# A dot-product modulation spread over three stages and block sums moved to VectorE, in a two-layer hybrid encoder

## The chip, the cores and the metric

The kernel runs on one core of one Trainium2 chip. The metric is the device time of one execution in microseconds; the reported time is the median of several runs. Below, PE is TensorE, DVE is VectorE, ACT is ScalarE, POOL is GpSimd, and SP issues most DMAs.

## The reference, cut to what matters

A two-layer encoder over 1024 positions and 1024 channels, all in float32. Each layer has a mixer (attention in the first, a long convolution called hyena in the second) and a feed-forward part. Six vectors per layer (shift, scale and gate of both parts) come from the conditioning vector c: the *modulation*.

```
mod[l]  = silu(c) @ ada_w[l] + ada_b[l]            # 6 vectors of 1024 per layer
h       = rmsnorm(x, norm1_g[l]) * (1 + scale1) + shift1
x       = x + gate1 * mixer(h)                     # layer 0: ... @ w_o; layer 1: hyena, w_in ... w_out
h       = rmsnorm(x, norm2_g[l]) * (1 + scale2) + shift2
g, v    = split(h @ w_up[l], 2)                    # 2 x 2816
x       = x + gate2 * ((silu(dwconv3(g)) * v) @ w_down[l])
```

## The kernel before, in words

Channels lie on the 128 partitions, positions along the free axis; tiles are 128x512 or 128x1024. A float32 product is done as three products of rounded parts: every operand is split into hi (a cast, on ACT) and lo (a subtraction, `sub_lo` L162, on DVE), and PE adds hi·hi, lo·hi and hi·lo. The order in which each engine issues its instructions is set by the Tile scheduler, which lays the program out with a simulated timeline; so an edit reorders the queues around it. Queues themselves run in order.

The stages, in us of the profile: qkv and attention to 620; the output product w_o (loop over `dt_`, L882 to L909; beside it `filter_mlp`, a small network for the hyena filter) to 708, then the norm; the first layer's **up projection** to 1194; its **down projection** to 1477, beside which the hyena filters are generated; the hyena mixer and w_out to about 2310; the second layer's up projection (2310 to 2740) and down projection (to the end).

An up projection has 22 row tiles f. The first two are computed plainly (L985 to L993). The other 20 are iterations of a Strassen-like scheme: two weight tiles `ga` and `va` of 128x1024 are loaded, four **block sums** of 128x512 halves (L1027 to L1030, on POOL) turn them into the operands of seven products, each operand is split by `fill` (ACT cast L1006, DVE subtraction L162), and 84 matmuls of 128x512 run. DVE adds the partial results (L1035 to L1059), does two thirds of the convolution of the gate (L288, L289), and closes the iteration with gate·v (`times`, L979), which is stored (`sg`).

Beside the first up projection runs `l1_work` (L1165), called through `extra` in slots of the loop: it prepares the second layer's hyena weights w_in and w_out, in 64 pieces of 128x512: load into one of three buffers `wi_raw` (LPB = 3, L1172), cast to `wi_hi` (one buffer, ACT L1190), subtract (DVE L1191, into wi_raw), store the lo part (L1192). The same generator does the first 16 of the 48 **dots** of the second layer's modulation: one dot (`mod_dot`, L197) multiplies a 128x1024 tile of ada_t, loaded by `mod_load` (L1153, 512 KB), by the row silu(c) in `ssq`, and accumulates along the free axis to one column of `mod`. Sixteen dots serve the second layer's first two vectors, the next 24 its third to fifth, the last 8 the gate of the feed-forward part. The other 32 dots run in the down projection (L1113), after an accumulation into x.

Of the kernel before, what the change touches and what calls it, by code (L numbers as in the profile page):

```python
# [7 lines left out]
F32 = mybir.dt.float32  # L8
F32R = mybir.dt.float32r
AF = mybir.ActivationFunctionType  # L10
# [43 lines left out]
L1_UP = 16  # L54
# [61 lines left out]
def tile_kernel(ctx: ExitStack, tc: tile.TileContext, t: dict):  # L116
# [75 lines left out]
    def silu_row(row):  # L192
        nc.sync.dma_start(row, t["c"].partition_broadcast(P))
        nc.scalar.activation(row, row, AF.Silu)
# [65 lines left out]
    class Weights:  # L260
# [8 lines left out]
        def load(self, src, lo=None):  # L269
            return load_split(src, self.pool(), 1, lo_src=lo)  # L270
# [63 lines left out]
    def filter_mlp(S, new_ps):  # L334
# [31 lines left out]
        yield  # L366

# [463 lines left out]
    def pst(nm):  # L831
        ycnt[0] += 1
        n = sum(YB[0:len(Y)])
        return Y[(ycnt[0] - 1) % n // 2].tile([P, L], F32, name=nm, tag="y")
# [46 lines left out]
    mlp = filter_mlp(scratch, lambda: pst("mlp_ps"))  # L881
    for dt_ in range(KT):  # L882
        w = wt.load(t["w_o"][dt_]) if dt_ else w_o0
        nc.sync.dma_start(x[dt_], t["x"][dt_])
        if dt_ < 5:
            yp = pst("wo_y")
            for k in range(KT):
                for hf in range(2):
                    wo_mm(yp[:, HS[hf]], w, hf, k)
            for hf in range(2):  # L890
                res(yp[:, HS[hf]], x[dt_], mod[:, 0, 2, dt_:dt_ + 1], HS[hf], dt_ == 0, sq_tile(sp_))
            nc.sync.dma_start(xsd[0][dt_], x[dt_])
        else:
            wl3 = (wl3 if dt_ > 5 else []) + [w]
        next(mlp, None)
    for _ in mlp:
        pass
# [49 lines left out]
    def ffn(l, base, work, tail, more=None):  # L947
# [63 lines left out]
        for f in range(NPL[l], NF):  # L1011
# [8 lines left out]
            G = nc.gpsimd  # L1020
# [6 lines left out]
            G.tensor_tensor(s1, a21, a22, op=ADD)  # L1027
            G.tensor_tensor(a21, a11, a21, op=SUB)
            G.tensor_tensor(a11, s1, a11, op=SUB)
            G.tensor_tensor(a12, a12, a11, op=SUB)  # L1030
# [52 lines left out]
        dots = mod_dots(L1_UP, 48, tp_) if l == 0 else None  # L1083
# [13 lines left out]
        for j in range(len(ends) - 1):  # L1097
# [3 lines left out]
            for dt_ in range(KT):  # L1101
# [10 lines left out]
                V.scalar_tensor_tensor(x[dt_], yp, gate[dt_], x[dt_], op0=MUL, op1=ADD)  # L1112
                if l == 0 and (j == 0 or cnt % 2 == 0):  # L1113
                    next(dots, None)
# [49 lines left out]

    def l1_work(pool, after):  # L1165
# [10 lines left out]
        dots = mod_dots(0, L1_UP)  # L1176
        lo_load(0)
        n = d = 0
        for i in range(L1_STEPS):
            while d < (i + 1) * L1_UP // L1_STEPS:  # L1180
                next(dots)
                d += 1
# [525 lines left out]
    ffn(1, "right", "left", tail1)  # L1708
# [129 lines left out]
```

## Time and profile before

| | |
|---|---|
| median of 3 runs | 2998.22 us (2996.7 to 3005.12) |
| the profiled execution's own time | 2999.89 us |
| its span | 2998.1 us |
| mean granted TensorE clock | 0.979 |
| PE busy | 2834.4 us, 95% |
| DVE busy | 2289.6 us, 76% |
| ACT busy | 1228.0 us, 41% |
| POOL busy | 536.2 us, 18% |
| DMA moved | 438.44 MB, mean 146 GB/s |

An engine is busy while one of its instructions runs; the share is an average over stages with different limits. Idle time is put down to the semaphore that came last. The chain of waits is followed back from the end to what released each step. The granted clock is what the throttle gave TensorE as a share of 2.4 GHz.

### The profile page before, as it was taken

To read this page: it belongs to the slowest core of one execution; us is meant where nothing else is said; L and a number is where in the kernel's file an instruction comes from. 1 tells how busy PE (TensorE), PEld (TensorE's weight loads), DVE (VectorE), ACT (ScalarE), POOL (GpSimd) and SP (SyncE) were. 2 spreads that over 40 slices of the span, in tenths; PEclk is the share of its full clock that TensorE was granted. 3 is DMA by queue.
4 is the path that set the end of the run, shared out by engine and by line. 5 is a ranking of instruction groups with operands and counts; after the bars stand their busy time and mean duration, and the time that the engine had idled before them with its cause. 6 is when DMAs were issued, how large, how long until landed. Compare 5 with 4: busy or idle time off the path is not lost.

```text
span 2998.1 us, 36517 instructions
## 1 busy us (share of the span) xinstructions
PE 2834.4 (95%) x13152; PEld 2309.0 (77%) x13152; DVE 2289.6 (76%) x3017; ACT 1228.0 (41%) x1998; POOL 536.2 (18%) x452
## 2 busy tenths in 40 slices
PE   5989999999899999999889999999988999999998
PEld 4867777777677787888677878887866888887887
DVE  7788989856997776997667886788976867667544
ACT  3558888833444333334332232323333433333211
POOL 0064465200322232001000000000000323320000
PEclk9999999999999999999989999999998999999999
DMA  6252222132776423975446664665656222223321
GB/s 230 76 170 57 57 64 64 43 129 71 263 235 229 151 84 115 296 249 170 141 158 205 200 217 156 205 204 190 205 183 223 78 85 84 85 77 129 131 84 57
DMA packets 222040, 438.44 MB, mean 146 GB/s; under 512 B 21826, under 2 KB 116834, under 8 KB 217380
## 3 DMA queue, kind: packets, MB, share of 16 engines
q1 hardware_dynamic: 190052, 406.75, 40.1%
q0 software_dynamic: 31808, 29.37, 4.3%
q8 instruction: 104, 1.70, 0.2%
q14 instruction: 76, 0.62, 0.1%
HBM read 307.05 MB, written 128.99 MB: 145 GB/s over the span
## 4 chain that ended last, share of the span: by engine, by line
PE 72%; DVE 13%; DMA 9%; issue 3%; ACT 2%; POOL 1%; SPq 0%; DVEq 0%; ACTq 0%; POOLq 0%
PE w_ps L919 19%; PE d_ps L181 16%; PE u_ps L1278 6%; PE pt_ps L732 3%; PE wo_y L181 3%; PE ab_ps L1414 2%; PE qkv_mm L181 2%; PE o_ps L750 2%; PE o_ps L751 2%; PE s_ps L708 2%; PE s_ps L709 2%; PE g_ps L283 2%; DMA wld<-wi_raw 1%; PE f_ps L462 1%; PE f_ps L463 1%
## 5 line engine op out<-in xcount | busy, mean ns | idle before, releaser
L162 DVE TENSOR_TENSOR w_lo<-u,w_hi 128x1024 fp32r<-128x1024 f32 x120 | 180.5, 1505 | 62.6 <-ACT w_hi L1006 62.6
L1006 ACT CAST w_hi<-u 128x1024 fp32r<-128x1024 f32 x120 | 125.9, 1050 | 209.7 <-PE w_ps L919 204.1
L162 DVE TENSOR_TENSOR pT_lo<-pt_ps,pT_hi 128x512 fp32r<-128x512 f32 x256 | 167.9, 682 | 47.6 <-ACT pT_hi L737 45.5
L181 PE MATMUL d_ps<-s_lo,wd_hi 128*128 128x512 f32 x608 | 195.2, 390 | 0.0
L181 PE MATMUL d_ps<-s_hi,wd_lo 128*128 128x512 f32 x608 | 193.9, 390 | 0.0
L181 PE MATMUL d_ps<-s_hi,wd_hi 128*128 128x512 f32 x608 | 193.7, 391 | 0.0
L919 PE MATMUL w_ps<-t_h,w_hi 128*128 128x512 f32 x480 | 191.2, 398 | 2.5 <-ACT w_hi L1006 1.3
L919 PE MATMUL w_ps<-t_l,w_hi 128*128 128x512 f32 x480 | 190.5, 397 | 0.0
L919 PE MATMUL w_ps<-t_h,w_lo 128*128 128x512 f32 x480 | 189.1, 395 | 0.6 <-DVE w_lo L162 0.6
L1112 DVE SCALAR_TENSOR_TENSOR xd<-d_ps,mod,xd 128x1024 f32<-128x1024 f32 x104 | 132.8, 1281 | 67.8 <-PE d_ps L181 67.5
L737 ACT CAST pT_hi<-pt_ps 128x512 fp32r<-128x512 f32 x256 | 144.9, 588 | 71.3 <-PE pt_ps L732 64.5
L716 DVE TENSOR_REDUCE nmx<-s_ps 128x1 f32<-128x1024 f32 x128 | 155.6, 1217 | 12.8 <-PE s_ps L709 10.8
L732 PE MATMUL pt_ps<-ident,p_t 128*128 128x128 f32 x1024 | 154.2, 274 | 10.3 <-DVE pT_lo L162 9.3
L732 PEld LDWEIGHTS pt_ps<-ident,p_t 128*128 128x128 f32 x1024 | 126.5, 141 | 45.3 <-DVE pT_lo L162 7.7
L919 PE MATMUL w_ps<-fh_h,w_hi 128*128 128x512 f32 x320 | 127.6, 399 | 19.5 <-ACT w_hi L1006 14.6
L726 ACT ACTIVATE p_t<-s_ps,nmx 128x1024 f32<-128x1024 f32 x128 | 143.7, 1124 | 3.1 <-DVE nmx L716 1.9
L1278 PE MATMUL u_ps<-fh_h,w_lo 128*128 128x512 f32 x384 | 140.3, 421 | 2.2 <-DMA w_lo<-wld 2.2
L1027 POOL TENSOR_TENSOR s<-u 128x512 f32<-128x512 f32 x40 | 53.9, 1347 | 487.6 <-DVE w_lo L162 221.5
L1278 PE MATMUL u_ps<-fh_l,w_hi 128*128 128x512 f32 x384 | 136.3, 418 | 1.8 <-DVE fh_l L239 1.8
L1278 PE MATMUL u_ps<-fh_h,w_hi 128*128 128x512 f32 x384 | 131.4, 416 | 3.4 <-ACT fh_h L238 3.4
L181 PEld LDWEIGHTS d_ps<-s_hi,wd_hi 128*128 128x128 f32 x608 | 113.7, 188 | 24.0 <-issue 0.9
L181 PEld LDWEIGHTS d_ps<-s_lo,wd_hi 128*128 128x128 f32 x608 | 113.7, 188 | 23.2 <-issue 0.4
(394 smaller groups left out, 7686.4 us busy)
## 6 DMA issues: line engine op xcount, KB each, us to landing
u<-in_w_up_dram SPq DMA_DIRECT2D x80, 512.0 KB
w_raw<-in_w_down_dram SPq DMA_DIRECT2D x44, 512.0 KB
sg<-gate SPq DMA_DIRECT2D x40, 512.0 KB
w_raw<-sg SPq DMA_DIRECT2D x40, 512.0 KB
w_raw<-in_ada_w_dram SPq DMA_DIRECT2D x32, 512.0 KB
m_raw<-in_ada_t_dram SPq DMA_DIRECT2D x32, 512.0 KB
ed<-eo SPq DMA_DIRECT2D x64, 256.0 KB
eo<-ed SPq DMA_DIRECT2D x16, 1024.0 KB
```

The costliest lines, as they stand in the source:

```text
L162: V.tensor_tensor(lo, src, hi.bitcast(F32), op=SUB)
L181: mm(out[:, cs], lhsT=a, rhs=b[:, cs], start=start and i == 0, stop=stop and i == 2)
L283: mm(pp[:, HS[hf]], lhsT=(wh, wh, wl)[i][:, ks], rhs=hd[hf][i % 2][k], start=k == 0 and i == 0, stop=k == n - 1 and i == 2)
L708: mm(s_ps[:, cs], lhsT=qg[u][:, i], rhs=kTh[g][:, cs], start=True, stop=False)
L716: V.tensor_reduce(nmx, s_t[u, i], op=ALU.max, axis=AX.X, negate=True)
L726: nc.scalar.activation(p_t, s_ps, AF.Exp, bias=nmx, accum_out=sums[u][:, i:i + 1])
L732: nc.tensor.transpose(tp[:, i * P:(i + 1) * P], pts[u, i][:, sb * P:(sb + 1) * P], ident)
L737: nc.scalar.copy(ph, pt_t[u, sb][0])
L919: mm(out, lhsT=(w[0], w[0], w[1])[i][:, k * P:(k + 1) * P], rhs=b[i % 2][k], start=k == 0 and i == 0, stop=k == 3 and i == 2)
L1006: nc.scalar.copy(w[0], src)
L1112: V.scalar_tensor_tensor(x[dt_], yp, gate[dt_], x[dt_], op0=MUL, op1=ADD)
L1278: mm(yp[:, HS[hf]], lhsT=(wh, wh, wl)[i][:, k * P:(k + 1) * P], rhs=hd[hf][i % 2][k], start=k == 0 and i == 0, stop=k == KT - 1 and i == 2)
```

## The change

Three things move. The first 16 dots leave the first up projection for the w_o loop: the new `wide_dots` does two per `dt_`, each as two halves of 128x512 (two accumulators, added at the end of eight), with three buffers of halves taken from `scratch`, the still unused tiles of the second half of h. The next 24 stay in the down projection but are pinned: `tc.issue_after` puts each behind the accumulation of an odd `dt_` in DVE's order. The last 8 go into the second layer's up projection, one per slot of `extra` (`l1_mod5`), on `w_raw` tiles. And the four block sums per iteration are issued on DVE instead of POOL, in both layers.

```diff
--- before.py
+++ after.py
@@ -51,7 +51,7 @@
 LPB = 3
 DPR = (4,4)
 EXN = 3
-L1_UP = 16
+L1_WO, L1_DN = 16, 40
 L1_STEPS = 54
 EOB = 3
 G_END = 32
@@ -364,6 +364,30 @@
             nc.sync.dma_start(ad[0][:, HS[hf]], S[2 + hf])
             nc.sync.dma_start(ad[1][:, HS[hf]], sf[hf])
         yield
+
+    def wide_dots(S, n):
+        row, bufs = S[0:2], [S[2:4], S[4:6], S[6:8]]
+        part = const.tile([P, n], F32, name="m_part")
+        for hf in range(2):
+            nc.sync.dma_start(row[hf], t["c"][:, HS[hf]].partition_broadcast(P))
+            nc.scalar.activation(row[hf], row[hf], AF.Silu)
+
+        def load(j):
+            for hf in range(2):
+                nc.sync.dma_start(bufs[j % 3][hf], t["ada_t"][2 + j // KT, j % KT][:, HS[hf]])
+        load(0)
+        load(1)
+        for j in range(n):
+            if j + 2 < n:
+                load(j + 2)
+            i, k = divmod(j, KT)
+            for hf, acc in enumerate((mod[:, 1, i, k:k + 1], part[:, j:j + 1])):
+                w = bufs[j % 3][hf]
+                V.scalar_tensor_tensor(w, w, 1.0, row[hf], op0=MUL, op1=MUL, accum_out=acc)
+            if k == KT - 1:
+                V.tensor_tensor(mod[:, 1, i], mod[:, 1, i], part[:, j - k:j + 1], op=ADD)
+                mod_bias(1, i)
+            yield
 
     JS = ((4, 1), (2, 3), (0, 7), (6, 5))
 
@@ -879,6 +903,7 @@
 
     scratch = hd[1][0] + hd[1][1]
     mlp = filter_mlp(scratch, lambda: pst("mlp_ps"))
+    dots = wide_dots(scratch[7:], L1_WO)
     for dt_ in range(KT):
         w = wt.load(t["w_o"][dt_]) if dt_ else w_o0
         nc.sync.dma_start(x[dt_], t["x"][dt_])
@@ -893,6 +918,8 @@
         else:
             wl3 = (wl3 if dt_ > 5 else []) + [w]
         next(mlp, None)
+        for _ in range(L1_WO // KT):
+            next(dots)
     for _ in mlp:
         pass
     hd[1] = new_h(h_pools[1], "fh")
@@ -1017,17 +1044,16 @@
             cv = op.tile([P, 2, L], F32, name="cv", tag="cv", bufs=CVB)
             s1 = op.tile([P, 512], F32, name="s1", tag="s1", bufs=1)
             pu = op.tile([P, 2, 512], F32, name="pu", tag="pu", bufs=1)
-            G = nc.gpsimd
             w1, w2 = fill(ga, 0)
             product(w1, B11, y1_[:, 0:512])
             nc.scalar.copy(pu[:, 0], y1_[:, 0:512])
             product(w2, B21, y2[:, 0:512])
             if late:
                 late()
-            G.tensor_tensor(s1, a21, a22, op=ADD)
-            G.tensor_tensor(a21, a11, a21, op=SUB)
-            G.tensor_tensor(a11, s1, a11, op=SUB)
-            G.tensor_tensor(a12, a12, a11, op=SUB)
+            V.tensor_tensor(s1, a21, a22, op=ADD)
+            V.tensor_tensor(a21, a11, a21, op=SUB)
+            V.tensor_tensor(a11, s1, a11, op=SUB)
+            V.tensor_tensor(a12, a12, a11, op=SUB)
             w6, w3 = fill(ga, 1)
             w5, = fill(s1, 3)
             w7, w4 = fill(va, 2)
@@ -1080,7 +1106,7 @@
                 mm3(yp, wh[:, ds], wl[:, ds], sh[:, cs], sl[:, cs], i == 0, i == len(grp) - 1)
 
         wdt = None
-        dots = mod_dots(L1_UP, 48, tp_) if l == 0 else None
+        dots = mod_dots(L1_WO, L1_DN, tp_) if l == 0 else None
         ends = [NF0 + sum(gr[:i]) for i in range(len(gr) + 1)]
 
         def load_to(n, free):
@@ -1109,9 +1135,10 @@
                 else:
                     yp = pst("d_ps")
                     down(yp, dt_, slice(0, L), grp)
-                V.scalar_tensor_tensor(x[dt_], yp, gate[dt_], x[dt_], op0=MUL, op1=ADD)
-                if l == 0 and (j == 0 or cnt % 2 == 0):
-                    next(dots, None)
+                ins = V.scalar_tensor_tensor(x[dt_], yp, gate[dt_], x[dt_], op0=MUL, op1=ADD)
+                if l == 0 and dt_ % 2:
+                    with tc.issue_after(ins.ins):
+                        next(dots, None)
                 if l == 0 and j:
                     cnt += 1
                     if cnt % FGD == 0 and wdt is None and next(fgen, 1):
@@ -1162,6 +1189,11 @@
                 mod_bias(1, i // KT)
             yield
 
+    def l1_mod5(pool, after):
+        V.tensor_copy(ssq[0:1, 0:1], after[0:1, 0:1].bitcast(F32))
+        silu_row(ssq)
+        yield from mod_dots(L1_DN, 48)
+
     def l1_work(pool, after):
         los = [(t["w_in"][i], wld[i], cs) for i in range(24) for cs in HS]
         los += [(t["w_out"][i], wold[i], cs) for i in range(KT) for cs in HS]
@@ -1173,13 +1205,9 @@
 
         V.tensor_copy(ssq[0:1, 0:1], after[0:1, 0:1].bitcast(F32))
         silu_row(ssq)
-        dots = mod_dots(0, L1_UP)
         lo_load(0)
-        n = d = 0
+        n = 0
         for i in range(L1_STEPS):
-            while d < (i + 1) * L1_UP // L1_STEPS:
-                next(dots)
-                d += 1
             while n < (i + 1) * len(los) // L1_STEPS:
                 src, dst, cs = los[n]
                 n += 1
@@ -1705,7 +1733,7 @@
             V.scalar_tensor_tensor(o_t, x[k][:, HS[hf]], col(C_FG + k), rs, op0=MUL, op1=MUL)
             nc.sync.dma_start(t["out"][k][:, HS[hf]], o_t)
 
-    ffn(1, "right", "left", tail1)
+    ffn(1, "right", "left", tail1, l1_mod5)
     wt.release()
     Y[0].release()
```

Over the whole program PE has the same 12246 instructions in its order, DVE 160 block sums and 32 half dots more and 16 whole dots less, POOL 160 sums less, SP 32 loads of 256 KB in place of 16 of 512 KB, and two halves and one whole row of c more.

Line numbers of the changed kernel are shifted: L1053 to L1056 are the block sums, L1006 is gate·v (L979 before), L1219 the lo-part subtraction (L1191 before), L1061, L1062, L1065, L1076 and L1078 the partial results (L1035, L1036, L1039, L1050, L1052 before).

DVE, first layer, first iteration of the up loop, before: the dots (L197) among the lo-part subtractions (wi_raw) and the w_lo of the products.

```order
L1191 TENSOR_TENSOR wi_raw<-wi_raw,wi_hi 128x512
L162 TENSOR_TENSOR w_lo<-u,w_hi 128x1024
L197 SCALAR_TENSOR_TENSOR w_raw,mod<-w_raw,ssq 128x1024
L1191 TENSOR_TENSOR wi_raw<-wi_raw,wi_hi 128x512
L197 SCALAR_TENSOR_TENSOR w_raw,mod<-w_raw,ssq 128x1024
L162 TENSOR_TENSOR w_lo<-u,w_hi 128x1024
L1191 TENSOR_TENSOR wi_raw<-wi_raw,wi_hi 128x512
L197 SCALAR_TENSOR_TENSOR w_raw,mod<-w_raw,ssq 128x1024
```

The same place with the change:

```order
L1219 TENSOR_TENSOR wi_raw<-wi_raw,wi_hi 128x512
L162 TENSOR_TENSOR w_lo<-u,w_hi 128x1024
L1219 TENSOR_TENSOR wi_raw<-wi_raw,wi_hi 128x512
L1055 TENSOR_TENSOR u<-s_7811,u 128x512
L1056 TENSOR_TENSOR u<-u 128x512
L1053 TENSOR_TENSOR s_7948<-u 128x512
L1219 TENSOR_TENSOR wi_raw<-wi_raw,wi_hi 128x512
L1054 TENSOR_TENSOR u<-u 128x512
L162 TENSOR_TENSOR w_lo<-u,w_hi 128x1024
L1219 TENSOR_TENSOR wi_raw<-wi_raw,wi_hi 128x512 x2
L162 TENSOR_TENSOR w_lo<-u,w_hi 128x1024
L1219 TENSOR_TENSOR wi_raw<-wi_raw,wi_hi 128x512
```

The dots are gone; subtractions of the split pieces and block sums stand where they stood. Between the closing products before and after this iteration there are 13 split pieces, seven before.

DVE, first layer, a later iteration, before: it begins with its gate·v.

```order
L979 TENSOR_TENSOR gate<-gate,cv 128x1024
L162 TENSOR_TENSOR w_lo<-u,w_hi 128x1024
L1191 TENSOR_TENSOR wi_raw<-wi_raw,wi_hi 128x512
L1035 TENSOR_TENSOR cv<-pu,w_ps 128x512
L1036 TENSOR_TENSOR pu<-pu,w_ps 128x512
L1191 TENSOR_TENSOR wi_raw<-wi_raw,wi_hi 128x512
L162 TENSOR_TENSOR w_lo<-u,w_hi 128x1024
L1191 TENSOR_TENSOR wi_raw<-wi_raw,wi_hi 128x512
L1039 TENSOR_TENSOR pu<-pu,w_ps 128x512
L162 TENSOR_TENSOR w_lo<-s_8794,w_hi 128x512
L1050 TENSOR_TENSOR cv<-pu,w_ps 128x2x512
L1052 TENSOR_TENSOR pu<-pu,w_ps 128x512
```

With the change, an iteration of the same kind:

```order
L1006 TENSOR_TENSOR gate<-gate,cv 128x1024
L1219 TENSOR_TENSOR wi_raw<-wi_raw,wi_hi 128x512
L1056 TENSOR_TENSOR u<-u 128x512
L1061 TENSOR_TENSOR cv<-pu,w_ps 128x512
L1062 TENSOR_TENSOR pu<-pu,w_ps 128x512
L1219 TENSOR_TENSOR wi_raw<-wi_raw,wi_hi 128x512
L162 TENSOR_TENSOR w_lo<-u,w_hi 128x1024
L1219 TENSOR_TENSOR wi_raw<-wi_raw,wi_hi 128x512
L1065 TENSOR_TENSOR pu<-pu,w_ps 128x512
L162 TENSOR_TENSOR w_lo<-s_8848,w_hi 128x512
L1053 TENSOR_TENSOR s_9001<-u 128x512
L1076 TENSOR_TENSOR cv<-pu,w_ps 128x2x512
```

The block sums stand between the split pieces and the evictions. Such an iteration had seven split pieces; in the eight iterations after the first there are now 6, 6, 6, 7, 6, 7, 6 and 7, in the tenth none.

DVE, second layer, entry of the up loop, before:

```order
L979 TENSOR_TENSOR gate<-gate,v_ps 128x1024
L289 SCALAR_TENSOR_TENSOR gate<-g_ps,cols,gate 128x1023
L162 TENSOR_TENSOR w_lo<-s_19789,w_hi 128x512
L979 TENSOR_TENSOR gate<-gate,v_ps 128x1024
L162 TENSOR_TENSOR w_lo<-u,w_hi 128x1024 x3
L162 TENSOR_TENSOR w_lo<-s_19903,w_hi 128x512
L1035 TENSOR_TENSOR cv<-pu,w_ps 128x512
```

With the change:

```order
L1006 TENSOR_TENSOR gate<-gate,v_ps 128x1024
L289 SCALAR_TENSOR_TENSOR gate<-g_ps,cols,gate 128x1023
L197 SCALAR_TENSOR_TENSOR w_raw,mod<-w_raw,ssq 128x1024 x2
L1053 TENSOR_TENSOR s_19787<-u 128x512
L1006 TENSOR_TENSOR gate<-gate,v_ps 128x1024
L1054 TENSOR_TENSOR u<-u 128x512
L162 TENSOR_TENSOR w_lo<-s_19787,w_hi 128x512
L197 SCALAR_TENSOR_TENSOR w_raw,mod<-w_raw,ssq 128x1024
L1055 TENSOR_TENSOR u<-s_19787,u 128x512
L162 TENSOR_TENSOR w_lo<-u,w_hi 128x1024
L197 SCALAR_TENSOR_TENSOR w_raw,mod<-w_raw,ssq 128x1024
L162 TENSOR_TENSOR w_lo<-u,w_hi 128x1024
```

Ahead of the first w_lo of u there are now three dots (of the eight), three sums and the w_lo of s; in the order before, the first w_lo of u followed the closing products directly, the sums being on POOL.

## Rows read from the trace of the kernel before

**Rows 1.** The page's first lines: the span, and for each engine its busy us, share of the span and count of instructions.

```profile
span 2998.1 us, 36517 instructions
...
PE 2834.4 (95%) x13152; PEld 2309.0 (77%) x13152; DVE 2289.6 (76%) x3017; ACT 1228.0 (41%) x1998; POOL 536.2 (18%) x452
```

**Rows 2.** Windows of the whole kernel, core 0; each row is a stretch (us from the span's start) and its length, then for each engine its busy us and its count of instructions, then the granted TensorE clock, the DMA engines' mean busy share and GB/s.

```profile
core 0: us, PE busy (x) PEld busy (x) DVE busy (x) ACT busy (x) POOL busy (x), PEclk, DMA share, GB/s
600.00:700.00 100.00, 96.83 (x435) 75.78 (x434) 50.38 (x78) 31.88 (x50) 2.27 (x4) 0.98 0.34 121
760.00:780.00 20.00, 15.85 (x65) 11.50 (x64) 20.00 (x21) 8.44 (x11) 11.60 (x6) 1.00 0.71 239
800.00:820.00 20.00, 14.08 (x52) 10.14 (x50) 20.00 (x24) 6.48 (x10) 7.77 (x4) 0.91 0.83 284
900.00:920.00 20.00, 17.40 (x70) 13.96 (x69) 15.77 (x17) 9.05 (x12) 5.26 (x4) 0.91 0.66 207
1040.00:1060.00 20.00, 20.00 (x90) 16.57 (x89) 14.57 (x15) 6.46 (x7) 6.99 (x5) 1.00 0.24 79
1200.00:1300.00 100.00, 100.00 (x487) 84.21 (x486) 95.72 (x128) 34.54 (x51) 9.57 (x18) 1.00 0.90 291
2400.00:2500.00 100.00, 100.00 (x435) 81.28 (x434) 70.03 (x68) 33.19 (x36) 30.24 (x21) 1.00 0.25 86
```

**Rows 3.** Timeline of DVE at the gate·v products (L979) that close an iteration of the first up projection: start us, duration us, instruction. The first row closes the two tiles before the loop, the others iterations 1, 4, 10, 11 and 20 of 20.

```profile
764.80 1.22 DVE L979 TENSOR_TENSOR gate<-gate,v_ps 128x1024 f32<-128x1024 f32 x1
...
810.85 1.22 DVE L979 TENSOR_TENSOR gate<-gate,cv 128x1024 f32<-128x1024 f32 x1
...
867.47 1.22 DVE L979 TENSOR_TENSOR gate<-gate,cv 128x1024 f32<-128x1024 f32 x1
...
1004.03 1.21 DVE L979 TENSOR_TENSOR gate<-gate,cv 128x1024 f32<-128x1024 f32 x1
...
1019.78 1.82 DVE L979 TENSOR_TENSOR gate<-gate,cv 128x1024 f32<-128x1024 f32 x1
...
1191.70 1.22 DVE L979 TENSOR_TENSOR gate<-gate,cv 128x1024 f32<-128x1024 f32 x1
```

**Rows 4.** Chain of waits, followed back within 910 to 952 us, some two iterations of the first up projection: start us, length us, what it is. wld<-wi_raw is a store of a lo part, wi_raw<-in_w_in a load of a half tile of w_in.

```profile
916.61 6.03 DMA wld<-wi_raw
...
922.65 4.06 DMA wi_raw<-in_w_in_dram
...
928.16 2.68 DMA wld<-wi_raw
...
931.24 3.50 DMA wld<-wi_raw
...
934.75 3.79 DMA wi_raw<-in_w_in_dram
...
940.80 6.16 DMA wld<-wi_raw
```

**Rows 5.** The dots of the first up projection, all instructions of tile w_raw on DVE from 690 to 1180 us: shortest/median/longest ns, first and last start, shape; and what DVE sat idle for before them (us, times).

```profile
L197 DVE SCALAR_TENSOR_TENSOR w_raw<-w_raw,ssq x16: 1209/1218/2315, 761.9 to 823.7; 128x1024 f32<-128x1024 f32 x16
...
  DMA w_raw<-in_ada_t_dram: 2.5, 1
```

**Rows 6.** Timelines of POOL (first two rows) and of DVE (the others) in the first iteration of the first up projection: start us, duration us, instruction.

```profile
772.43 2.27 POOL L1027 TENSOR_TENSOR s<-u 128x512 f32<-128x512 f32 x1
774.78 2.15 POOL L1028 TENSOR_TENSOR u<-u 128x512 f32<-128x512 f32 x1
...
773.49 2.30 DVE L162 TENSOR_TENSOR w_lo<-u,w_hi 128x1024 fp32r<-128x1024 f32 x1
...
777.41 1.21 DVE L162 TENSOR_TENSOR w_lo<-u,w_hi 128x1024 fp32r<-128x1024 f32 x1
...
779.69 0.68 DVE L1191 TENSOR_TENSOR wi_raw<-wi_raw,wi_hi 128x512 fp32r<-128x512 f32 x1
780.29 1.22 DVE L197 SCALAR_TENSOR_TENSOR w_raw<-w_raw,ssq 128x1024 f32<-128x1024 f32 x1
```

**Rows 7.** Groups of instructions by line, 2400 to 2700 us (second up projection), two of POOL's four block sums: busy us, mean ns | idle us before them and releaser.

```profile
L1030 POOL TENSOR_TENSOR u<-u 128x512 f32<-128x512 f32 x16 | 34.6, 2166 | 1.3
...
L1027 POOL TENSOR_TENSOR s<-u 128x512 f32<-128x512 f32 x16 | 20.6, 1288 | 110.6 <-DVE w_lo L162 110.6
```

**Rows 8.** Groups by line, 840 to 1010 us (the loaded iterations of the first up projection), DVE; same columns.

```profile
L1191 DVE TENSOR_TENSOR wi_raw<-wi_raw,wi_hi 128x512 fp32r<-128x512 f32 x50 | 41.9, 839 | 26.8 <-ACT wi_hi L1190 26.7
...
L979 DVE TENSOR_TENSOR gate<-gate,cv 128x1024 f32<-128x1024 f32 x8 | 16.3, 2034 | 0.0
```

**Rows 9.** Timeline of DVE in the w_o stage: one residual product of 128x512 with an operand in PSUM.

```profile
684.41 0.75 DVE L858 SCALAR_TENSOR_TENSOR xr<-wo_y,mod,xr 128x512 f32<-128x512 f32 x1 [3.24 <-PE wo_y L181]
```

**Rows 10.** Chain of waits from 680 to 712 us, the end of the w_o stage: the last matmuls of wo_y and the norm's matmul that follows.

```profile
697.22 5.80 PE wo_y L181 x25
703.01 0.45 PE nrm L232 x4
```

**Rows 11.** Groups by line, 1190 to 1490 us (down projection of the first layer), DVE: the 32 dots there.

```profile
L197 DVE SCALAR_TENSOR_TENSOR m_raw<-m_raw,ssq 128x1024 f32<-128x1024 f32 x32 | 39.0, 1219 | 4.0 <-DMA m_raw<-in_ada_t_dram 4.0
```

**Rows 12.** Timeline of DVE where the second layer's up projection enters its loop.

```profile
2351.52 1.28 DVE L289 SCALAR_TENSOR_TENSOR gate<-g_ps,cols,gate 128x1023 f32<-128x1023 f32 x1
2352.71 0.68 DVE L162 TENSOR_TENSOR w_lo<-s,w_hi 128x512 fp32r<-128x512 f32 x1
2353.92 1.22 DVE L979 TENSOR_TENSOR gate<-gate,v_ps 128x1024 f32<-128x1024 f32 x1 [0.53 <-ACT gate L975]
2355.06 6.42 DVE L162 TENSOR_TENSOR w_lo<-u,w_hi 128x1024 fp32r<-128x1024 f32 x3
```

**Rows 13.** All 64 lo-part subtractions of the first up projection (L1191): shortest/median/longest ns, first and last start.

```profile
L1191 DVE TENSOR_TENSOR wi_raw<-wi_raw,wi_hi x64: 674/686/1774, 775.7 to 1002.5; 128x512 fp32r<-128x512 f32 x64
```

## The prediction

> **What bounds the kernel now.** Four views, read in this order. The page's first lines say that PE works for 2834.4 of 2998.1 us and DVE for 2289.6 [rows 1]: only about 164 us exist in which PE is not busy, and a change that leaves its matmuls alone can win nothing else. The windows say where some of these lie [rows 2]. In the second layer's up projection PE has no hole (100.00 of 100 us, 435 matmuls), nor between 1200 and 1300 in the down projection. In the first layer's up projection it does: 65 matmuls in 760 to 780, 52 in 800 to 820, 70 in 900 to 920, against 90 in an undisturbed 20 us (1040 to 1060). The granted clock is 0.91 in the windows with the largest holes, 1.00 elsewhere; its cost is inside the iterations' lengths below.
>
> How long an iteration takes there is read from the product gate·v (L979), which closes an iteration on DVE [rows 3]. From 1019.78 to 1191.70 there are nine iterations without extra work: **19.1 us** each, PE's own pace. From 867.47 to 1004.03 there are six, each with seven lo-part splits: 136.56 / 6 = **22.8 us**, or 3.25 us for a split (42 of them). Between 810.85 and 867.47 three iterations carry five splits each and take 18.9 us: five are free, seven are not. The first (764.80 to 810.85) takes 46.05 us with seven splits and most of the first 16 dots.
>
> What paces the seven is told by the chain of waits [rows 4]: store of a lo part (6.03 us), load into the freed buffer (4.06), store (2.68), store (3.50), load (3.79), store (6.16). It is a ring of three buffers, each of which goes through a load, a cast, a subtraction and a store before the next load may start, and ACT's in-order queue holds the w_hi of the product behind it. DMA is busy 0.66 of the time meanwhile, so it is the trip and not the bandwidth. The first iteration is another matter: the dots are all done by 825 us [rows 5], DVE is busy 20.00 of 20 us [rows 2], and one dot lets it wait 2.54 us for its 512 KB of ada_t.
>
> **First up projection: one number decides.** Call p the time per split. The order of DVE puts 13 splits between the first two of these closing products now (seven before), then 6, 6, 6, 7, 6, 7, 6, 7 in the next eight iterations, 64 in all, and none in the tenth, which carried seven. As long as the ring paces, the first iteration takes 13p and the next eight 51p; the tenth falls to 19.1. Before, these ten took 46.05 + 193.18 us (764.80 to 1004.03), 239.23. So the stage changes by 64p + 19.1 - 239.23 = 64p - 220.1. With today's p of 3.25 this is **-12.1 us**: the splits start earlier, because the dots no longer stand among them.
>
> What moves p? The 160 block sums leave POOL. A DVE subtraction of a w_lo takes 2.30 us while a sum runs on POOL (773.49 beside 772.43 and 774.78) and 1.21 at 777.41 [rows 6]; the sums themselves take 1.29 to 2.17 in the mean [rows 7]. In the loaded iterations the split's subtraction averages 839 ns [rows 8], 680 without a neighbour [rows 6] (seven of these: 1.1 us), and the closing product 2034 [rows 8] instead of 1220 (0.8 us) [rows 3]: 1.9 us an iteration of slowed DVE work, directly ahead of stores of the chain, comes free. In exchange DVE gets four sums of 128x512 an iteration. Nothing of that shape with both operands in SBUF is longer than 0.68 when alone, and the next instruction starts 0.60 later (779.69 to 780.29) [rows 6]: 2.4 us. If all four stand in front of a late split the net is +0.5 an iteration, if none does it is -1.9; the order puts them between splits, some before PE's evictions, where DVE has 4 to 5 us of idle time in 20. I take -0.4, for nine iterations -3.6 us, nearest to the row in which PE, not DVE, has the wait. That is p = 3.19; the ends are 3.32 and 2.98 (below that PE's 19.1 us binds).
>
> The Trainium skill (SBUF — State Buffer, section "SBUF: two separate sides") says that VectorE with two SBUF operands and GpSimd exclude each other for a whole instruction, the loser blocking fully. The 1.1 us by which the w_lo grows agrees with that. By the rule alone each of four sums could have cost DVE its own length, 1.3 us, or 5.2 us an iteration for the 2.4 paid, and the stage would go to PE's floor.
>
> **The w_o stage: +1.5 us.** 32 half dots are added to DVE, each at most the 0.75 us that a 128x512 product with a PSUM operand takes [rows 9]: 24 us. DVE is busy 50.38 of 100 us there, DMA 0.34 [rows 2], and PE's wo_y is the chain (5.80 us of it up to 703, before the norm) [rows 10]. Their 8.5 MB stand in SP's queue among the x, w_o and w_up loads, three buffers of halves deep, so SP can wait for a dot there. If all is hidden it costs nothing. If the last pair stands in front of the sum of squares and of the norm, it costs 1.5 us, twice 0.75; if SP is late with one w_o load, 4. I take 1.5, since the norm ends this stage and DVE is in order.
>
> **Down projection: 0.** 24 dots instead of 32, 39.0 us in all before [rows 11], on a DVE with PE at 100.00 beside it. The pin behind odd accumulations spaces them; behind a pinned dot stand the next splits of s and w_d, which have a ring of their own. Cover gone, one dot is 1.2 us; 0 to 2.
>
> **Second up, entry: +4.5 us.** Eight dots (1.14 us from start to start: 9.2) and the sums of the first iterations stand in DVE's queue where today POOL has the sums ready before 2352: w_lo of s runs at 2352.71, the three w_lo of u from 2355.06 [rows 12], and PE does not stop. Now between the gating at 2351.52 and the first w_lo of u stand two dots, then a sum, the closing product, a sum, the w_lo of s, a dot and a sum: 1.2 + 2.3 + 0.6 + 1.14 + 0.6 + 0.6 + 1.14 + 0.6 = 8.2 us, so 2359.7, **4.6 us later** than 2355.06. PE needs it for the second third of its first products. From zero (PE does the other products first) to 9 (the next w_lo, behind two dots more and with the clock down). Later iterations there gain and lose nothing: DVE had 70 of 100 us, PE stays full.
>
> **Sum.** -12.1 - 3.6 + 1.5 + 0 + 4.5 = -9.7 us. The profiled execution took 2999.89 us (span 2998.1), so 2990.2; the median of three runs, 2998.22, lies 1.7 lower, which gives **2988.5**. In p: the whole change is 64p - 214.1. At 3.205 it is -9, at 3.35 nothing, at 3.49 +9. (0.3%, 9 us, is about what a measurement of this kernel can tell from no change.)
>
> **Rivals.**
> - **PE's pace throughout** (p = 2.98): nine iterations at 19.1, and the first, whose closing products lie two of PE's iterations apart, at 38.2 to 39: 64 x 2.98 - 214.1 = -23.4, so 2975. For it: five splits are free at 18.9 us, so six at 19.5 are near; what POOL's sums cost DVE may be more than the two rows show, as the page above has it. Against: the chain is mostly DMA, and nothing takes a load or store of the ring away from 825 us on. 0.20.
> - **The ring trips exactly as before, or a little slower** (p from 3.25 to 3.45): the sums cost what POOL's company cost. 2992 at 3.25, 2998 at 3.35, 3005 at 3.45. For it: the trips of 2.7 to 6.2 us are set by what else is queued on DMA, which is unchanged. 0.23.
> - **Slower: DVE becomes the pacer.** Its in-order queue now carries PE's block sums behind subtractions that wait for DMA (wi_hi late): a late load then delays a21 and a11 and with them PE's w_hi, which POOL used to make ready regardless. DVE's work of a loaded iteration is 17.9 of 22.8 us (15.77 in 20 [rows 2]); less 1.9 and one split (0.6), plus 2.4, it is 17.8 of 19.5 us, leaving 1.7 for waits, where it idles 4.9 now. It decides from p = 3.49 on (a six-split iteration of 20.9 us); with the 3.60 that the whole 64 average today from first to last (775.7 to 1002.5 us [rows 13]) it is +16, 3014. 0.15.
> - The forecast itself, p between about 3.1 and 3.25: 2982 to 2993. 0.42.
>
> **Numbers.** Faster by more than 9 us: the first rival and some two thirds of the forecast, 0.48. Slower: the last rival and the slow edge of the second, 0.17. The same: 0.35. The range runs from just below PE's floor with a free entry (2971) to p = 3.45 with an entry that costs a little more, 3006.
>
> **What would show it.** Right: closing products of the first up 19 to 20 us apart with six splits and 22 with seven, the last split before 980 us, PE unbroken an iteration earlier (about 988 instead of 1004); w_lo of u at 1.2 us throughout; a PE hole of 3 to 6 us just after the second up begins, none later; the w_o stage at most 2 us longer. Wrong: DVE at 19 or more of 20 us from 820 on, holes of PE released by a21 or a11 on DVE, or holes in the w_o stage released by loads.

## The result, and the profile after

The change made the kernel slower: 3008.09 us (7 runs, 3006.47 to 3010.45) against 2999.06 us (7 runs, 2996.31 to 3005.12); the ratio is 1.0025, 95% interval 1.0015 to 1.0036. It is the recorded ratio of undisturbed runs, so it need not be the quotient of the two medians (1.0030). The profiled execution took 3006.47 us, its span is 3004.7.

Lengths of the stages, each from the first to the last start of its matmuls in the trace (us; the first down projection from its first matmul with u to the last of u with wd_hi in its tail, the second from its first to its last matmul with s; e1, e3, e4 and e5 are experiments below):

| stage | before | after | e1 | e3 | e4 | e5 |
|---|---|---|---|---|---|---|
| w_o, from the last o_ps on | 90.6 | 90.4 | 90.6 | 90.5 | 91.5 | 90.5 |
| first up projection, loop | 422.5 | 421.1 | 420.3 | 408.6 | 419.6 | 409.2 |
| first down projection | 321.6 | 316.4 | 318.0 | 317.7 | 323.5 | 316.6 |
| second up projection, loop | 390.2 | 396.2 | 396.0 | 390.2 | 390.2 | 383.3 |
| second down projection | 219.7 | 219.7 | 219.7 | 219.7 | 219.7 | 219.7 |

So the forecast's main gain, 15.7 us in the first up projection, came out as 1.4 (between the closing products, which the forecast used, 428.1 us in place of 426.9); the loss at the second's entry came about as forecast. Of the span's +6.6, 5.1 us lie ahead of w_o (the last o_ps at 622.6 in place of 617.5) and 1.7 between the last wo_y and the first matmul of the first loop, which no row of the table counts: 58.3 us in place of 56.6, with PE waiting 3.48 us in place of 0.68 for the first w_hi of the loop. Up to w_o every queue has the order it had before. Yet the qkv stage ends between 194.6 and 194.9 us in the three profiles of the kernel before and its variants (e2, e8) and between 195.0 and 199.2 in the eleven of the changed kernel and its variants; what makes these up to 4 us is not shown.

The windows of after, columns as in [rows 2]:

```profile
600.00:700.00 100.00, 96.18 (x425) 74.09 (x426) 69.11 (x148) 31.57 (x53) 4.67 (x7) 1.00 0.58 215
760.00:780.00 20.00, 16.52 (x66) 13.05 (x65) 16.58 (x22) 11.73 (x16) 0.00 (x0) 0.91 0.70 238
800.00:820.00 20.00, 14.61 (x57) 11.48 (x56) 15.48 (x21) 7.90 (x11) 0.00 (x0) 0.83 0.60 206
900.00:920.00 20.00, 17.90 (x78) 14.26 (x76) 16.41 (x23) 8.49 (x13) 0.00 (x0) 1.00 0.69 231
1040.00:1060.00 20.00, 20.00 (x88) 16.28 (x87) 15.85 (x19) 7.09 (x9) 0.00 (x0) 1.00 0.24 79
...
2400.00:2500.00 100.00, 100.00 (x434) 81.31 (x433) 75.41 (x86) 34.73 (x38) 0.00 (x0) 1.00 0.23 79
```

Three things are to be seen. DVE is no longer full at 760 to 820 (16.58 and 15.48 of 20 us; 20.00 before), yet PE has the same holes (66 and 57 matmuls). At 900 to 920 DVE works for 16.41 us and idles for 3.6: it is not full, where the forecast's slow rival made it the pacer. And at 1040 to 1060, where PE is busy for 20.00 of 20 us at a clock of 1.00 and waits for nothing, it does **88 matmuls in place of 90**.

The closing products of the first up projection (L1006; [rows 3] before): the two tiles ahead of the loop, iterations 1, 4, 10 and 20.

```profile
768.72 1.22 DVE L1006 TENSOR_TENSOR gate<-gate,v_ps 128x1024 f32<-128x1024 f32 x1
...
809.96 1.22 DVE L1006 TENSOR_TENSOR gate<-gate,cv 128x1024 f32<-128x1024 f32 x1
...
878.25 1.22 DVE L1006 TENSOR_TENSOR gate<-gate,cv 128x1024 f32<-128x1024 f32 x1
...
1003.22 1.22 DVE L1006 TENSOR_TENSOR gate<-gate,cv 128x1024 f32<-128x1024 f32 x1
...
1196.82 1.22 DVE L1006 TENSOR_TENSOR gate<-gate,cv 128x1024 f32<-128x1024 f32 x1
```

The first iteration takes 41.2 us (46.05 before; 13p at 3.19 was 41.5), as forecast. Iterations 2 to 9 take 22.0 us in the mean, and their length does not follow the number of splits: the five with six splits take 20.8 to 25.0 us, the three with seven 20.6 to 21.7, where 19 to 20 and 22 were forecast. The trace of before shows the same: its three iterations with five splits, 18.9 us in the mean, take 21.6, 16.0 and 19.1. And the ten iterations after the tenth take 193.6 us, 187.7 before, without a single split in them; 3.1 of these 5.9 us are gone in e1 (190.5), and the rest is made up in the tenth iteration, which is 5.6 us shorter than before. Each 1.22 in the rows is the closing product without POOL beside it, 2034 ns before [rows 8]: that relief came in full.

The splits, with the DVE idle time ahead of them, in the loaded iterations (columns as in [rows 8]), and the chain of waits there ([rows 4] before):

```profile
L1219 DVE TENSOR_TENSOR wi_raw<-wi_raw,wi_hi 128x512 fp32r<-128x512 f32 x42 | 28.8, 685 | 22.6 <-ACT wi_hi L1218 22.5
```

```profile
834.32 8.04 DMA wld<-wi_raw
842.37 4.16 DMA wi_raw<-in_w_in_dram
...
859.32 5.24 DMA wld<-wi_raw
864.58 2.73 DMA wi_raw<-in_w_in_dram
```

The subtraction is at its 685 ns, but loads and stores of the ring still stand in the chain, and a trip through the ring is longer: from one load's issue to the issue of the load three splits later 10.6 us for 10.0 before (mean of splits 11 to 58). First to last split is 771.0 to 985.4 us, p = 214.4 / 63 = 3.40.

The entry of the second up projection on DVE ([rows 12] before), and PE's one hole there:

```profile
2351.86 1.28 DVE L289 SCALAR_TENSOR_TENSOR gate<-g_ps,cols,gate 128x1023 f32<-128x1023 f32 x1
2353.05 1.22 DVE L197 SCALAR_TENSOR_TENSOR w_raw<-w_raw,ssq 128x1024 f32<-128x1024 f32 x1
...
2357.67 0.69 DVE L162 TENSOR_TENSOR w_lo<-s,w_hi 128x512 fp32r<-128x512 f32 x1
...
2360.02 1.22 DVE L162 TENSOR_TENSOR w_lo<-u,w_hi 128x1024 fp32r<-128x1024 f32 x1
```

```profile
2365.26 0.68 PE L946 MATMUL w_ps<-t_h,w_hi 128*128 128x512 f32 x1 [3.96 <-ACT w_hi L1033]
```

The first w_lo of u comes at 2360.02 (2359.7 was worked out) in place of 2355.06, and PE waits 3.96 us, here for a w_hi.

### The profile page after: what moved, and what is told of

It is laid out like the page before. It is cut to its first block, busy times and chain, and to the rows that moved or that the text cites. A ratio compares the mean times of both kernels' runs of the same rounds, so it can differ in the third digit from the quotient of the medians.

```text
span 3004.7 us, 36415 instructions
## 1 busy us (share of the span) xinstructions
PE 2837.0 (94%) x13152; PEld 2308.3 (77%) x13152; DVE 2333.3 (78%) x3212; ACT 1231.0 (41%) x2001; POOL 289.1 (10%) x292
## 4 chain that ended last, share of the span: by engine, by line
PE 55%; DVE 8%; DMA 8%; issue 2%; ACT 1%; SPq 0%; DVEq 0%; ACTq 0%; POOLq 0%
PE w_ps L946 20%; PE d_ps L181 16%; PE u_ps L1306 6%; PE ab_ps L1442 2%; DMA wld<-wi_raw 2%; PE f_ps L486 1%; PE f_ps L181 1%; PE f_ps L487 1%; PE z_ps L1420 1%; PE z_ps L1421 1%; DMA wi_raw<-in_w_in_dram 1%; DMA rd<-fw 1%; PE wout_y L181 1%; PE g_ps L283 1%; PE wout_y L1593 1%
## 5 line engine op out<-in xcount | busy, mean ns | idle before, releaser
L162 DVE TENSOR_TENSOR w_lo<-u,w_hi 128x1024 fp32r<-128x1024 f32 x120 | 146.6, 1222 | 60.2 <-ACT w_hi L1033 60.1
L181 PEld LDWEIGHTS d_ps<-s_hi,wd_lo 128*128 128x128 f32 x608 | 113.6, 188 | 23.8 <-issue 0.9
L1442 PE MATMUL ab_ps<-prod,dfti 128*128 128x256 f32 x512 | 124.8, 387 | 7.1 <-DVE prod L1512 3.2
```

The source lines that it names most:

```text
L162: V.tensor_tensor(lo, src, hi.bitcast(F32), op=SUB)
L181: mm(out[:, cs], lhsT=a, rhs=b[:, cs], start=start and i == 0, stop=stop and i == 2)
L1442: mm(ap[:, i], lhsT=dfti[:, m, :], rhs=v, start=n == 0, stop=n == len(ops) - 1)
```

## The experiments

Theory A: the new tile m_part, 64 bytes beside the constants, moves the tiles above it on the left side of SBUF by 64 bytes, and some matmuls run slower for it. Theory B: order alone. C, E, F: the block sums on DVE cost, by their time or by their places. D: the ring's trip paces whatever DVE does. Times are medians; ratios are to runs of the kernel before, with their 95% intervals.

**e1: m_part out of the way.**

```diff
-        part = const.tile([P, n], F32, name="m_part")
+        part = scol.rearrange("p o k -> p (o k)")
```

> The changed kernel, but the 16 second accumulators lie in scol, an existing tile, in place of the new 64-byte tile m_part; every queue keeps its order, and the tiles left of the middle of SBUF go back by 64 bytes to where they lay before. Theory A (placement): the matmuls of the first up projection that read the differences t start 227 ns after one another again in place of 233, those of wo_y 227 in place of 231; the first up projection loses 5 to 6 us and wo_y 1, so 3001 to 3003 us against 3008, unless the wait for the filters at the end of the down projection takes the gain back (then 3006 to 3008 with the same spacing of 227). Theory B (order alone is to blame): spacing and time as in the changed kernel, 3007 to 3009.

Measured: 2999.87 us, ratio 1.0004 (0.9994 to 1.0014). The matmuls of the differences t in the part of the first up projection where PE waits for nothing (1021 to 1180 us), in after and in e1: count, shortest/median/longest ns, first and last start.

```profile
L946 PE MATMUL w_ps<-t_h,w_hi x100: 394/394/394, 1021.2 to 1178.0; 128*128 128x512 f32 x100
```

```profile
L946 PE MATMUL w_ps<-t_h,w_hi x102: 389/389/389, 1021.2 to 1179.4; 128*128 128x512 f32 x102
```

A matmul's duration overlaps the next one's, so the price is read from starts. In after, ten steps take 2.33 us, 233 ns each (226.7 in e1 and before: 1062.76 to 1065.03 in the trace of before are also ten steps):

```profile
1066.53 0.39 PE L946 MATMUL w_ps<-t_l,w_hi 128*128 128x512 f32 x1
...
1068.86 0.39 PE L946 MATMUL w_ps<-t_h,w_lo 128*128 128x512 f32 x1
```

With every queue in the same order, 64 bytes cost 0.21% (1.0025 against 1.0004). Theory A holds on spacing (wo_y too: 227.8 ns for 231.3) and on time. The profiled up projection fell by 0.8 us only, not 5 to 6. Compared step by step (a step is the time from one matmul's start to the next), with the 13152 matmuls of both traces in the same order, after's steps of under 0.3 us in the loop add up to 5.6 us more than e1's and its longer steps to 4.9 us less: there the slower matmuls hide in PE's holes. Over the whole trace the short steps add up to 8.5 us more (4.2 in the differences, 1.4 in the loop's other matmuls, 1.2 in wo_y) and the longer ones to 8.4 less, in a pair that is the slowest of e1's runs (3005.07 us) and the fastest of after's. Between e5 and e12 below, whose matmuls have the same pace, the short steps differ by 0.3 us. So the slower steps suffice for the loss in the medians; how much of it is theirs this pair cannot tell.

**e2: the tile alone.** The kernel before with 64 bytes beside its constants that nothing uses.

```diff
+    pad = const.tile([P, 16], F32, name="pad")
+    nc.vector.memset(pad, 0.0)
```

> The kernel before with one unused tile of 64 bytes beside its constants, which moves the left side of SBUF by 64 bytes as m_part does; order unchanged. Theory A (placement): matmuls of the differences in the first up projection at 233 ns in place of 227, 5 to 7 us more: 3004 to 3007 us. Theory B: no difference, 2998 to 3000.

Measured: 3006.74 us, ratio 1.0023 (1.0013 to 1.0033); first up projection 425.7 us against 422.5.

In before and in e2:

```profile
L919 PE MATMUL w_ps<-t_h,w_hi x103: 389/389/389, 1020.8 to 1180.0; 128*128 128x512 f32 x103
```

```profile
L921 PE MATMUL w_ps<-t_h,w_hi x100: 394/394/394, 1020.6 to 1180.0; 128*128 128x512 f32 x100
```

394 again, with nothing else of the change. The slower pace is shown from both sides. Of the loop's 3.2 us, 2.8 are its last nine iterations, without splits, at 0.3 us each. The twelve runs lie between 2998.01 and 3009.91 us, and this profile is of the shortest, so its stages do not show the 7 us of the median; compared step by step with before as above, its short steps add up to 9.0 us more, its longer ones to 10.0 less.

**e3: the sums back on POOL.** As e1, with

```diff
-            V.tensor_tensor(s1, a21, a22, op=ADD)
+            nc.gpsimd.tensor_tensor(s1, a21, a22, op=ADD)
...
```

> As e1_part_in_scol, with the four block sums back on POOL in both layers. If the sums in DVE's queue set the pace of the loaded iterations (theory C), time per split falls from 3.40 to 3.25 or less and the first up projection gains another 5 to 10 us against e1; if the ring of three buffers does (theory D), it stays at 3.3 to 3.5 and the stage within 3 us. In the second up projection the entry loses 1 to 2 us in place of 6 if sums and dots together make the loss. Total 2994 to 2999 by C, 2998 to 3002 by D.

Measured: 2986.46 us, ratio 0.9958 (0.9946 to 0.9970): faster than the kernel before by 0.42%. First up projection 408.6 us against 420.3, second 390.2 against 396.0; the splits run from 766.2 to 963.0, p = 3.12. What SP waits for from 764 to 1005 us (us in total, times, longest), in e1 and in e3:

```profile
SPq L1204 <- DMA wld<-wi_raw: 77.6, 38, 5.6
...
SPq L1204 <- DMA wold<-wi_raw: 25.6, 12, 3.6
```

```profile
SPq L1204 <- DMA wld<-wi_raw: 50.1, 42, 2.9
...
SPq L1204 <- DMA wold<-wi_raw: 13.1, 13, 2.4
```

Theory C: moving the sums to DVE costs 0.46%. The scheduler lays the queues anew with it: e3 has 12, 7, 7, 6, 7, 7, 7, 7 and 3 splits in its first nine iterations, and PE's order differs from e1's in 916 of 13152 places, so the 0.46% are those of the sums together with that order. Against before, with the dots out of the first up projection, e3 gains 13.9 us there.

SP waits 103 us for the ring's stores with the sums on DVE, 63 with them on POOL, but that wait is no price: in e7 below it is 123 us and the stage is 10 us shorter than in e1. Where the ring's trip grows is read from the starts in the two traces (means of splits 11 to 58): from a load's issue to that of the load three splits later 10.7 us in e1, 9.5 in e3. Of the 1.2 us, 0.6 lie between the end of the subtraction and the store's issue on SP (0.79 against 0.21), 0.4 between that and the next load's issue (4.07 against 3.66), and 0.2 between cast and subtraction, where DVE's queue can hold a split back (0.63 against 0.42).

**e4: no dots in the second up projection** (as e1, with 32 pinned dots in the down projection).

```diff
-L1_WO, L1_DN = 16, 40
+L1_WO, L1_DN = 16, 48
```

> As e1_part_in_scol, with the last eight dots in the down projection of the first layer (32 there, none in the second up projection). The hole at the second up projection's entry (4.0 us on one w_hi, stage 6.0 us longer) shrinks to 0 to 2 if the dots make it (their 9.2 us stand ahead of w_lo), and stays at 3 or more if the sums do. The down projection takes eight dots more, 0 to 5 us at its end. Total against e1: -4 if the dots make the hole and the down projection hides them, 0 otherwise.

Measured: 3002.08 us, ratio 1.0012 (1.0003 to 1.0021). The second up projection is back at 390.2 us and PE's hole gone, with the sums still on DVE. In e3 it was gone too, with the dots still there: only both together make it. The down projection took back 5.5 us, so neither total came: 2 us more than e1, with intervals that overlap.

**e5: the second layer placed like the first.** As e3, with

```diff
+        if l:
+            V.memset(tpool.tile([P, 120], F32, name="phase")[:, 0:1], 0.0)
         db = tpool.tile([P, 4], F32, name="db", tag="db")
```

> As e3_sums_on_pool, with 480 unused bytes ahead of the second layer's difference tiles, which puts them at the same place modulo 512 bytes as the weights (480; they lay at 0). Order unchanged. Theory A (placement of the moving operand against the weights): the matmuls of the differences in the second up projection go from 233.6 to 227 ns, 720 of them, 5 us, and those of h perhaps from 228.8 to 227, 2 us more: 2979 to 2982 us. If placement is not what made the 233 ns, 2985 to 2988.

Measured: 2981.9 us, ratio 0.9944 (0.9932 to 0.9957). The same matmuls in the second layer, 2400 to 2700 us, before and in e5:

```profile
L919 PE MATMUL w_ps<-t_h,w_hi x184: 393/396/399, 2402.6 to 2695.6; 128*128 128x512 f32 x184
```

```profile
L946 PE MATMUL w_ps<-t_h,w_hi x191: 389/389/389, 2401.7 to 2697.3; 128*128 128x512 f32 x191
```

191 matmuls where there were 184, and the stage 383.3 us in place of 390.2: 6.9 us, where the two terms of the expectation add up to 7. PE was busy for 100.00 of 100 us here all along.

**e6: thin sums.**

```diff
-            V.tensor_tensor(a21, a11, a21, op=SUB)
+            V.tensor_tensor(a21[:, 0:64], a11[:, 0:64], a21[:, 0:64], op=SUB)
...
```

> As e1_part_in_scol (sums on DVE), but three of the four block sums work on 64 of their 512 columns, so seven eighths of these sums are left out; DVE is freed of about 1.6 us an iteration. Theory E (the sums' time on DVE sets the loaded iterations): time per split falls from 3.44 to 3.1 to 3.2, first up projection 408 to 412 us in place of 420, second 390 to 391 in place of 396. Theory F (their places in DVE's order, whatever they take): both stages within 2 us of e1.

Measured: 2992.34 us, ratio 0.9984 (0.9974 to 0.9994); first up projection 412.2 us, second 393.6, splits from 767.1 to 963.2, p = 3.11. Theory E fits the splits and some 8 of the 11.7 us; in the second up projection e6 gives back 2.4 of 5.8. The scheduler put seven splits into most iterations here, so places moved too: how much is the sums' time and how much their places is not separated.

**e7: four ring buffers**, sums on DVE.

```diff
-LPB = 3
+LPB = 4
```

> As e1_part_in_scol (sums on DVE), with four ring buffers for the lo parts in place of three. If the ring's trip through DMA sets the pace (theory D), the time per split falls below 3.2 and the first up projection to 405 to 412 us; if DVE's queue does (theory E), it stays at 417 to 421.

Measured: 2995.61 us, ratio 0.9989 (0.9980 to 0.9998); first up projection 410.5 us, splits from 770.8 to 973.2, p = 3.21; second up unchanged at 396.0. Theory D, within its stage; p misses "below 3.2" by a hair. SP's wait for the ring's stores is longer here than in e1, as said under e3:

```profile
SPq L1204 <- DMA wld<-wi_raw: 98.7, 41, 5.1
SPq L1204 <- DMA wold<-wi_raw: 24.0, 9, 4.5
```

With e6 this says where the sums cost: in the trip of a ring of three buffers. A fourth buffer gives 9.8 of the 11.7 us back with the sums still on DVE. Which of the trip's parts a sum lengthens first is argued from the means under e3, not shown.

**e8: the kernel before with its sums on DVE.**

```diff
-            G = nc.gpsimd
+            G = V
```

> The kernel before with the block sums on DVE and nothing else changed (dots as before). If the sums cost by themselves, whatever stands beside them, the first up projection goes from 422.5 to 430 to 434 us and the second stays at 390 (no dots there): 3006 to 3011. If they cost only through the new order of the splits and dots, 420 to 425 and 2997 to 3002.

Measured: 3008.36 us, ratio 1.0035 (1.0024 to 1.0046). First up projection 427.0 us, between the two expectations; second 390.2, no dots being there. The sums cost without the rest of the change too, less in the stage than without the dots (4.5 us against 11.7), perhaps since the dots already kept the splits back.

**e9: all together.** As e5, with four ring buffers.

> As e5_phase_layer2 (sums on POOL, both layers' tiles placed alike), with four ring buffers. If the ring still paces the first up projection at 3.1 us a split, the fourth buffer takes it to 400 to 405 us from 409, 2974 to 2978 in all; if PE or the order of DVE is the bound there by now, 407 to 410 and 2980 to 2983.

Measured: 2982.97 us, ratio 0.9943 (0.9930 to 0.9956), no better than e5; first up projection 412.9 us, outside both expectations, although the splits end at 948.0 (p = 2.84). With the sums on POOL a faster ring no longer shortens the stage; what bounds it then was not found.

**e10: no pin.** As e3, with

```diff
-                if l == 0 and dt_ % 2:
-                    with tc.issue_after(ins.ins):
-                        next(dots, None)
+                if l == 0 and (j == 0 or cnt % 2 == 0):
+                    next(dots, None)
```

> As e3_sums_on_pool, with the 24 dots of the down projection where the kernel before would put them (one after each accumulation of the first group, then one after every second), not pinned behind odd accumulations; they are all through by the middle of the stage. The stage, from the first matmul with u to the end of its tail, took 321.6 us before (32 dots, no pin), 317.7 in e3 (24, pinned), 323.5 in e4 (32, pinned). If the number of dots counts: 317 to 319 here. If the pin does: 321 to 323.

Measured: 2986.66 us, ratio 0.9959 (0.9947 to 0.9971); down projection 318.5 us. The number of dots counts; for the pin there is no sign.

**e11 and e12: which places are alike.** As e5, with `[P, 24]` (96 bytes) and `[P, 56]` (224 bytes) in place of `[P, 120]`; one run each.

> As e5_phase_layer2, with 96 unused bytes in place of 480: the second layer's difference tiles lie at 96 modulo 512, the weights at 480, which is 96 modulo 128. If only the place modulo 128 counts, their matmuls start 227 ns after one another as in e5; if the place modulo 512 (or 256) counts, 231 to 236.

> As e5_phase_layer2, with 224 unused bytes in place of 480: the second layer's difference tiles lie at 224 modulo 512, half a period from the weights' 480. If the place modulo 256 counts, their matmuls start 227 ns after one another as in e5; if only the place modulo 512 does, 231 to 236 as at 0, 64 and 96.

The differences' matmuls, 2400 to 2700 us, in e11 and in e12:

```profile
L946 PE MATMUL w_ps<-t_h,w_hi x189: 392/395/398, 2401.4 to 2699.8; 128*128 128x512 f32 x189
```

```profile
L946 PE MATMUL w_ps<-t_h,w_hi x191: 389/389/389, 2400.2 to 2695.8; 128*128 128x512 f32 x191
```

Spacing 233.0 ns in e11, 226.7 in e12; stage 388.6 and 383.3 us; time 2985.82 and 2980.49 us. A distance of 128 bytes between tile and weights (modulo 256) is slow, one of 256 is not.

## Why the prediction was wrong, point by point

- **"p = 3.19" is the step that failed**, in its part "What moves p". There the sums on DVE were booked at +0.5 to -1.9 us an iteration, taken as -0.4, so -3.6 us in the stage. They cost 11.7 us (e1 against e3), 1.3 in each of nine loaded iterations: 15 us of the miss. The relief was real (closing product 1.22, split 0.685) and did not help: freed and paid DVE time were set off against each other, as if DVE's busy time set the pace, but DVE idles 3.6 of 20 us, and what grew is the trip of a ring without slack, 10.7 us for 9.5 (e3, e6, e7).
- **One p for every split.** The whole stage was worked out as 64p. The first iteration came at 41.2 / 13 = 3.17, as forecast, the next eight at 176.0 / 51 = 3.45, and with six or seven splits they were equally long.
- **The dots' leaving: -12.1.** e3, with the sums on POOL, falls by 13.9 us. That it is so near is in part luck: e3 has 12 splits in its first iteration and p = 3.12, for which the forecast's formula gives -20, and its last ten iterations are 3.3 us longer than before.
- **A cost that no step had: placement.** The tile m_part was not in the sum at all. With its 64 bytes the kernel is slower by 0.21% (e1), and the kernel before by 0.23% (e2); that is more than the rest of the change comes to together. Two views of before could have spoken of it: the second layer ran 435 matmuls in 100 us with PE full, 4.35 in 1 us, the first 90 in 20, 4.5 [rows 2], with the same matmuls, and that difference was passed over.
- **The slow rival** (DVE becomes the pacer, p from 3.49 on) had the sign and, at 3.49, nearly the time, but by luck: DVE idles 3.6 of 20 us at p = 3.40, and without the placement the time is 2999.87 (e1).
- **The rival of the ring a little slower** (p from 3.25 to 3.45) had p, 3.40 here and 3.44 in e1, and with 2998 to 3005 for such a p also e1's time. Its ground, that the sums cost about what POOL's company cost, is too mild: they cost 11.7 us more.
- **PE's pace throughout, with the rule on the shared port.** It did not come: p is 3.40, not 2.98. The Trainium skill (SBUF — State Buffer, section "SBUF: two separate sides") has the loser of the pair block for the whole instruction. The w_lo at 1.22 us without POOL agrees; that the sums would therefore be worth moving does not follow, as e3 shows.
- **Second up, entry: +4.5.** Right: 5.8 to 6.0 us, the first w_lo of u at 2360.02 for 2359.7. It takes dots and sums together (e3, e4), which the forecast had added up.
- **w_o: +1.5.** The stage cost nothing to within 0.9 us: DVE 69.11 of 100 us, still covered. The 1.7 us lost behind it are not the norm's, as the forecast had it, but PE's wait for the loop's first w_hi.
- **Down projection: 0.** It gained 4 to 5 us, from eight dots fewer (e4, e10). The forecast took the full PE of 1200 to 1300 for the whole stage; between 1440 and 1480 PE was busy for 27.3 of 40 us before and for 31.2 after, and its waits for `eo`, an operand of the hyena filters, fell from 5.1 to 1.1 us.
- **Sum.** By ratios, which add up by construction: placement +0.21% (after against e1), sums on DVE +0.46% (e1 against e3), the dots' new places -0.42% (e3 against before), together +0.25%. Each is that of an edit with the order it brings. PE's order is not the same as before, although the section on the change reads so: 1761 of 13152 places hold another matmul, 963 of them in the up projections, and what that alone is worth was not tried.
- **The clock.** "0.91 in the windows with the largest holes" does not fit 760 to 780, with 15.85 us of PE at 1.00 [rows 2]; nothing in the sum rests on it.

## What to carry to other kernels

A tile added to a pool at the bottom of SBUF moves what lies above it on its side: compare the addresses of matmul operands before and after, and count matmuls per window where PE is full. When work is moved to an engine that stands inside a ring of few buffers, ask what it does to the ring's trip, not how busy the engine is. A mixed change is worth taking apart: here the dots alone, with the sums left on POOL and m_part out of the way, are faster by 0.42%, and with 480 bytes of padding by 0.56%.

## What the runs showed of the hardware that was not expected

The pace of fully overlapped 128x512 matmuls depends on where the moving operand lies against the weights in a partition. Places are bytes modulo 512, as the programs lay the tiles out. With both at 480 the matmuls start every 226.7 ns. With the moving tile at 0, 64 or 96 and the weights at 480 it is 233.0 to 234.1; with the tile at 480 and the weights at 32 it is 233.3; at 224, 256 bytes from the weights, it is 226.7 again. So of the distances tried, modulo 256, 0 is fast and 32, 96, 128 and 192 are slow; that 256 is the period rests on e12 alone, and why is not shown. Matmuls of h, whose tiles lie like their weights, are drawn in a little while those of the differences beside them are slow (227.5 to 229.0 ns) and are at 226.7 when they are not. The granted clock is 1.00 throughout. Other distances, and other shapes, were not tried.
